# Encoder block on one core: x normalised once into resident fp16 parts that every input product reads

## The chip, the core and the metric

The kernel runs on one core of a Trainium2 chip. The time is the device time of one execution in microseconds (us). Engines are named as the profile names them: PE is the matrix engine (TensorE), PEld its weight loads, DVE the vector engine, ACT the scalar engine, POOL GpSimd, SP the engine that issues most of the DMA transfers. On-chip memory is SBUF; matmul results land in PSUM, of which a "bank" here holds 128x512 fp32.

## What is computed

x is (1, 1024 tokens, 1024 channels). In the reference, cut to the parts that matter here:

```
xn = rmsnorm(x, norm_gain)
q, k, v_kv, gate_a, u, v, gate_b, merge = split(xn @ w_in)   # 512,128,128,512,512,512,512,2048
a = block_attention(axial_rope(rms(q)), axial_rope(rms(k)), v_kv) * silu(gate_a)
g = gelu(u) * (W_s @ layernorm(gelu(v)) + b) * silu(gate_b)
y = sigmoid(merge_a) * (a @ w_proj_attn) + sigmoid(merge_b) * (g @ w_proj_gmlp)
out = rmsnorm(x + y @ w_out, final_gain)
```

Everything is fp32 at the borders. Nearly every product is made of three matmuls on split operands: each operand is cut into a high part and a low part (value minus high part), and hi*hi, hi*lo and lo*hi are summed in PSUM (`mm3`). The parts are either fp32r (a rounded fp32 form that the matrix engine takes in one pass) or fp16.

## The kernel before, in words

The tile scheduler orders the instructions of each engine; source order and priorities steer it. The stages, in order of their first matmul on PE:

- **kv** (192 matmuls, 256 columns wide). `load_x` brings the eight 512 KB chunks of x transposed (`xT`), and for each makes `xh` on ACT (L158, x times gain, rounded to fp32r) and `xl` on DVE (L159). These sixteen tiles stay resident and are the x operand of kv, v, q, u, gate a and gate b. They are x times gain but not divided by the row's root mean square: that factor (`rstd`) is applied to the products later.
- **rstd**. `add_square` (L171) loads x again in its natural layout (`xn`, 8 x 512 KB) and sums squares on ACT. DVE and POOL turn the eight sums into `rstd` (L133, L134), at 43.8 to 46.1 us.
- **v** and **q** (192 matmuls of 512 columns each, L174 to L176). Weights are split by `nat_weights` (ACT hi L112, DVE lo L118). v takes part in the scheduler's choice while kv still runs, as it needs no `rstd`.
- **sp**, the spatial products of the gMLP branch, key and query norm and rotation, transposes into `kT` and `qT`.
- **Attention** (first scores at 135.7 us): 64 score steps (PE L550/L551, DVE maximum L553, ACT exp L557, ACT and DVE splits L563/L564 into fp16, then a DMA transpose), 32 mixes `o` (L576, fp16), and between them 24 **fill** halves: u, gate a (`ga`) and gate b (`gb`), 24 matmuls of 512 columns each (L488 to L490). Their weights come through `stream_w`: ACT hi, POOL lo (L118). After each fill DVE multiplies by `rB` (a tile with 0.5*rstd of each token in all partitions) straight from PSUM (L494, L511), then the gate's function follows.
- **yb** (gMLP projection), with the forms for the next stage prepared beside it: `x_chunk` normalises x once more (rB on DVE, L765) and splits sums of quarters of it into fp16 pairs (seven per chunk, four chunks).
- **g** (merge gates, fp16, first matmul at 450.1 us). Its weights are scaled to unit size by `unit_scale`: tiny PE matmul `usg`, ACT copy L673, four POOL steps L674 to L677, then ACT splits L682.
- **out** and the final norm, to 735 us.

Of the kernel before, what the change touches and what calls it, by code (L numbers as in the profile page):

```python
# [30 lines left out]
def hybrid_block_kernel(  # L31
# [133 lines left out]
    ssx = const([P, NT], "ssx")

    def add_square(tt):

# [2 lines left out]
        act.activation(xn, xn, AF.Square, accum_out=ssx[:, tt:tt + 1])  # L171

    def mm3(o, ah, al, bh, bl, start, stop):
        pe.matmul(o, ah, bh, start=start, stop=False)  # L174
        pe.matmul(o, ah, bl, start=False, stop=False)  # L175
        pe.matmul(o, al, bh, start=False, stop=stop)  # L176
# [62 lines left out]
    gsc = const([P, 2], "gsc")
    dve.tensor_scalar(out=gsc[:, 0:1], in0=ssp[:, 16:17], scalar1=2.0 ** -16, scalar2=1e-30, op0=ALU.mult, op1=ALU.add)  # L240
    pool.tensor_tensor(out=gsc[:, 0:1], in0=gsc[:, 0:1], in1=mhalf[:, 0:1], op=ALU.pow)
    dve.reciprocal(gsc[:, 1:2], gsc[:, 0:1])
    dve.tensor_scalar(out=gs, in0=gain, scalar1=gsc[:, 0:1], scalar2=None, op0=ALU.mult)
    rstd = const([P, NT], "rstd")
    power_rstd(rstd, ssx, NT, 1.0 / D)
    bmh = const([P, 16], "bmh")
    dve.tensor_scalar(out=bmh, in0=cs[:, C_BM:C_BM + 16], scalar1=0.5, scalar2=None, op0=ALU.mult)
# [791 lines left out]
```

## Time and profile before

| what | value |
|---|---|
| median of 3 runs | 736.73 us (736.58 to 737.26) |
| the profiled execution's own time | 736.99 us |
| its span (first to last instruction) | 735.2 us, so 1.8 us lie outside |
| PE busy | 714.0 us of the span (97%), 4633 matmuls |
| DVE / ACT / POOL busy | 565.9 / 431.2 / 110.4 us |
| mean granted clock of PE | 0.992 |

A row of a group reads: line, engine, operation, output<-inputs, shape, count | busy us, mean ns of one | idle time before it and what released it. A row of the timeline reads: start, duration, engine, line, operation, output<-inputs, shape, count, and in brackets the idle time before it with the instruction that ended it. [...] A row of the windows view reads: the window, its length, busy us (and instructions) of PE, PEld, DVE, ACT, POOL, the granted clock as a share of full speed, the DMA share and GB/s.

### The profile page before, as it was taken

The page shows a single profiled execution, that of the slowest core. Times are in us where ns is not written, and L with a number is a line of the kernel's source. Part 1 is how long each engine was busy: PE and PEld are TensorE (multiplying, and loading weights), DVE is VectorE, ACT ScalarE, POOL GpSimd, SP SyncE. Part 2 cuts the span into 40 slices and gives each one's busy share as a digit, 9 for nine tenths or more (in the row PEclk, how much of TensorE's full clock was granted, in tenths as well). Part 3 has the DMA queues.
Part 4 walks back from the last instruction along what each step waited for, and adds up shares of the span by engine and source line. Part 5 has one row for each costly group of instructions (what it writes and reads, how often), then busy time and mean ns, then how long its engine had stood idle before and what let it go on. Part 6 is the DMA issues. An engine that isn't in the chain of part 4 may idle for free.

```text
span 735.2 us, 11836 instructions
## 1 busy us (share of the span) xinstructions
PE 714.0 (97%) x4633; PEld 531.4 (72%) x4633; DVE 565.9 (77%) x822; ACT 431.2 (59%) x770; POOL 110.4 (15%) x101
## 2 busy tenths in 40 slices
PE   8999999998999999999999996999999999999996
PEld 8978888776777788788887883465464556488885
DVE  6556868799797988878789999888887898952223
ACT  6634564685797887777784775654455536621011
POOL 0011223133132232213200003001101110000000
PEclk9999999999999999999999998999999999999999
DMA  8830301054889999998999500130121005440202
GB/s 307 317 129 1 115 16 43 1 122 94 150 157 182 176 180 167 183 170 175 154 245 287 132 30 14 45 129 15 46 98 58 0 1 184 157 146 1 114 30 86
DMA packets 152904, 85.59 MB, mean 116 GB/s; under 512 B 135440, under 2 KB 136080, under 8 KB 152848
## 3 DMA queue, kind: packets, MB, share of 16 engines
q1 hardware_dynamic: 152560, 84.56, 46.6%
q8 instruction: 36, 0.59, 0.3%
q10 hardware_dynamic: 288, 0.28, 0.1%
q14 instruction: 20, 0.16, 0.1%
HBM read 47.07 MB, written 4.19 MB: 70 GB/s over the span
## 4 chain that ended last, share of the span: by engine, by line
PE 83%; DVE 5%; ACT 5%; DMA 5%; issue 1%; POOL 1%; SPq 0%; POOLq 0%; ACTq 0%; DVEq 0%
PE o L576 5%; PE out L175 4%; DMA T<-p 4%; PE out L176 4%; PE out L174 4%; PE s L550 3%; PE s L551 3%; PE g L174 3%; PE g L175 3%; PE g L176 3%; PE gb L488 2%; PE q L174 2%; PE q L175 2%; PE v L175 2%; PE v L174 2%; PE q L176 2%
## 5 line engine op out<-in xcount | busy, mean ns | idle before, releaser
L564 DVE SCALAR_TENSOR_TENSOR p<-P,ri,p 128x1024 f16<-128x1024 f32 x64 | 83.4, 1304 | 26.4 <-ACT p L563 26.3
L557 ACT ACTIVATE P<-s,nm 128x1024 f32<-128x1024 f32 x64 | 71.2, 1113 | 24.2 <-DVE nm L553 20.8
L563 ACT ACTIVATE p<-P,ri 128x1024 f16<-128x1024 f32 x64 | 73.1, 1145 | 15.7 <-DMA T<-p 8.8
L553 DVE TENSOR_REDUCE nm<-s 128x1 f32<-128x1024 f32 x64 | 77.6, 1214 | 3.0 <-PE s L551 2.9
L576 PEld LDWEIGHTS <-vS 128*64 128x64 f16 x1536 | 45.3, 111 | 19.0 <-issue 17.8
L576 PE MATMUL o<-T,vS 128*64 128x128 f16 x1536 | 52.0, 222 | 4.2 <-DMA T<-p 3.8
L118 POOL TENSOR_TENSOR wl<-wraw,wh 128x512 fp32r<-128x512 f32 x24 | 39.9, 1665 | 97.7 <-ACT wh L112 55.6
L550 PE MATMUL s<-kT,qT 128*128 128x512 f32 x128 | 52.9, 413 | 0.0
L551 PE MATMUL s<-kT,qT 128*128 128x512 f32 x128 | 50.9, 397 | 0.0
L911 ACT ACTIVATE sq<-xr 128x1024 f32<-128x1024 f32 x7 | 7.4, 1062 | 65.4 <-DVE xr L969 65.4
L969 DVE TENSOR_TENSOR xr<-out,xr 128x1024 f32<-128x1024 f32 x7 | 8.6, 1224 | 47.6 <-PE out L176 47.5
L674 POOL TENSOR_SCALAR scg<-scg 128x1 f32<-128x1 f32 x8 | 6.5, 807 | 206.7 <-ACT scg L673 206.6
L550 PEld LDWEIGHTS s<-kT,qT 128*128 128x128 f32 x128 | 24.3, 189 | 6.3 <-issue 0.2
L551 PEld LDWEIGHTS s<-kT,qT 128*128 128x128 f32 x128 | 24.3, 190 | 5.4 <-issue 0.2
L112 ACT CAST wh<-wraw 128x512 fp32r<-128x512 f32 x35 | 21.4, 616 | 10.4 <-PE ga L489 3.4
L682 ACT ACTIVATE wg<-graw,scg 128x512 f16<-128x512 f32 x16 | 11.4, 721 | 26.6 <-PE g L176 13.2
L488 PE MATMUL ga<-xh,wh 128*128 128x512 f32 x64 | 26.0, 406 | 0.8 <-DVE ga30w L494 0.5
L488 PE MATMUL u<-xh,wh 128*128 128x512 f32 x64 | 25.8, 402 | 0.0
L488 PE MATMUL gb<-xh,wh 128*128 128x512 f32 x64 | 25.5, 399 | 0.0
L175 PE MATMUL yb<-gml,wh 128*128 128x512 f32 x64 | 25.5, 398 | 0.0
L490 PE MATMUL u<-xh,wl 128*128 128x512 f32 x64 | 25.4, 397 | 0.0
L490 PE MATMUL gb<-xh,wl 128*128 128x512 f32 x64 | 25.4, 396 | 0.0
(554 smaller groups left out, 2143.9 us busy)
## 6 DMA issues: line engine op xcount, KB each, us to landing
wraw<-in_wall_dram SPq DMA_DIRECT2D x59, 256.0 KB, 3.4
graw<-in_wall_dram SPq DMA_DIRECT2D x16, 512.0 KB, 5.8
xraw<-in_xT_dram SPq DMA_DIRECT2D x13, 512.0 KB, 6.4
xn<-in_x_dram SPq DMA_DIRECT2D x8, 512.0 KB, 6.3
wor<-in_wall_dram SPq DMA_DIRECT2D x8, 512.0 KB, 5.1
xr<-in_x_dram SPq DMA_DIRECT2D x8, 512.0 KB, 3.8
out_dram<-xr SPq DMA_DIRECT2D x7, 512.0 KB, 2.6
xraw<-in_xT_dram SPq DMA_DIRECT2D x5, 256.0 KB, 5.5
```

The source lines that it names most:

```text
L174: pe.matmul(o, ah, bh, start=start, stop=False)
L175: pe.matmul(o, ah, bl, start=False, stop=False)
L176: pe.matmul(o, al, bh, start=False, stop=stop)
L488: pe.matmul(o, wh[:, C(dt % 4)], xh[dt][:, H(h)], start=(dt == 0), stop=False)
L490: pe.matmul(o, wl[:, C(dt % 4)], xh[dt][:, H(h)], start=False, stop=(dt == 7))
L550: pe.matmul(sp[:, H(hf)], qs, kT[:, 2 * v, H(hf)], start=True, stop=False)
L551: pe.matmul(sp[:, H(hf)], qs, kT[:, 2 * v + 1, H(hf)], start=False, stop=True)
L553: dve.tensor_reduce(out=nm, in_=sp, axis=AX.X, op=ALU.max, negate=True)
L557: act.activation(Pt, sp, AF.Exp, bias=nm, accum_out=rsum)
L563: act.activation(hi, Pt, AF.Copy, scale=ri)
L564: dve.scalar_tensor_tensor(out=lo, in0=Pt, scalar=ri, in1=hi, op0=ALU.mult, op1=ALU.subtract)
L576: pe.matmul(ot[64 * h:64 * h + 64, 0:128], vS[:, kt, v, 64 * vl:64 * vl + 64], T[:, h, 8 * p + kt, :], start=(n == 0), stop=(n == len(part ...
```

## The change

x is divided by its row norm once, before v, and kept as fp16 hi and lo parts (`x16`, eight tiles). v, q, u, ga, gb, and three of the seven forms of the g stage read these parts. Only kv still uses the unnormalised fp32r parts, which now live in short rings (F and G, three tiles each) instead of staying.

- **Squares.** The natural-layout loads of x and their ACT squares go. The transposed chunks are squared instead, chunks 0 and 2 on POOL and six on ACT; POOL and DVE add them into two tiles; eight one-column matmuls (`sst`) sum over partitions. `rstd` follows as before, and `rB` is now made at once, by eight 128-column matmuls (`rb`) and an ACT copy.
- **norm_all.** Eight times: DVE multiplies a chunk of x by gain and rB (`raw_part`, 1024 wide), ACT casts it to fp16, DVE subtracts for the low part. The splits of v's weights go between.
- **Weights.** v, q and fill weights become fp16 as well, scaled to unit size first. v: 8 loads, 8 ACT squares, `usv`, ACT copy, POOL steps, then ACT hi and DVE lo. q the same. Fill weights: `all_scales` loads all 24 halves once for ACT squares, makes twelve scales in one go, and each half is loaded again later and split (ACT hi, DVE lo; POOL no longer takes part).
- **Order of v.** Products of chunks 0 to 5 for six token tiles in three banks, then chunks 6 and 7 for these, then tiles 6 and 7.
- **After the fills** the multiplication by rB goes: `silu2` reads PSUM directly with a scale, `uw` becomes a scaled copy. q's head norm uses one scale instead of per-token `rsq` and `rstd`.
- **g stage.** Forms "11", "22", "21" are taken from x16, so `x_chunk` makes four fp16 pairs per chunk instead of seven.

The diff, cut to its core:

```diff
+    def add_square(dt):
+        t = t4("T16", f"xsq{dt}")
+        if dt in (0, 2):
+            pool.tensor_tensor(out=t, in0=xraw0[dt], in1=xraw0[dt], op=ALU.mult)
+        else:
+            act.activation(t, xraw0[dt], AF.Square)
...
+    with tc.high_priority():
+        power_rstd(rstd, sst[:, 0:NT], NT, 1.0 / D)
+        dve.tensor_scalar(out=rstdh, in0=rstd, scalar1=0.5, scalar2=None, op0=ALU.mult)
+        rp = ps_s("rb")
+        for tt in range(NT):
+            pe.matmul(rp[:, C(tt)], rstdh[:, tt:tt + 1].broadcast_to([P, P]), identr.bitcast(F32), start=True, stop=True)
...
+    def norm_all():
+        def raw_part(dt):
+            dve.scalar_tensor_tensor(out=xraw0[dt], in0=xraw0[dt], scalar=gs[:, dt:dt + 1], in1=rB, op0=ALU.mult, op1=ALU.mult)
+
+        wv.extend(nat_split(dt, rv, wv16, scv) for dt in range(2))
+        act.copy(rB, rp)
+        raw_part(0)
+        for dt in range(8):
+            if dt < 7:
+                raw_part(dt + 1)
+            t = sb.tile([P, 2, 1024], F16, tag="xr", bufs=BUFS["xr"], name=f"x16{dt}")
+            ia = act.copy(t[:, 0, :], xraw0[dt])
+            iv = dve.tensor_tensor(out=t[:, 1, :], in0=xraw0[dt], in1=t[:, 0, :], op=ALU.subtract)
+            x16.append(t)
+            if dt < 6:
+                wv.append(nat_split(dt + 2, rv, wv16, scv))
...
+    for dt in range(6):
+        for c in range(6):
+            nat_part(vsp[c // 2][:, H(c % 2)], dt, c, wv[dt])
...
+    def all_scales():
...
+                raw = load_w(W_TR + base[o[0]] + int(o[1]), h)
+                act.activation(raw, raw, AF.Square, accum_out=ss[:, i, h:h + 1])
...
+    def prep(k, et):
...
+            raw = load_w(W_TR + base[k] + et, i)
+            split16(t[:, i, 0, :], t[:, i, 1, :], raw, sc[0], "dve")
...
-    def silu2(zp, h, name):
-        w = t2(f"{name}w")
-        dve.tensor_tensor(out=w, in0=zp, in1=rB[:, H(h)], op=ALU.mult)
+    def silu2(zp, sc, name):
         t = t2(f"{name}t")
-        act.activation(t, w, AF.Tanh)
-        dve.scalar_tensor_tensor(out=t, in0=t, scalar=1.0, in1=w, op0=ALU.add, op1=ALU.mult)
+        act.activation(t, zp, AF.Tanh, scale=sc)
+        dve.scalar_tensor_tensor(out=t, in0=t, scalar=1.0, in1=zp, op0=ALU.add, op1=ALU.mult)
```

How the order moves, at the place that matters most, the passage from kv to v. (L numbers of the changed kernel are those of its own file: mm3 is L187 to L189 there.) On PE before, at the first v matmul; `xh`, `xl` are parts of x, `nh`, `nl` parts of v's weights, `wh`, `wl` of kv's:

```order
L175 MATMUL kv_90<-wl_182,xh_210 128x256
L176 MATMUL kv_90<-wh_181,xl_211 128x256
L174 MATMUL kv_89<-wh_247,xh_240 128x256
L174 MATMUL kv_90<-wh_247,xh_240 128x256
L174 MATMUL v_488<-nh_383,xh_95 128x512
L175 MATMUL kv_89<-wl_248,xh_240 128x256
L176 MATMUL kv_89<-wh_247,xl_241 128x256
L174 MATMUL kv_89<-wh_247,xh_240 128x256
```

PE now, at the end of kv:

```order
L188 MATMUL kv_93<-wl_340,xh_371 128x256
L189 MATMUL kv_93<-wh_339,xl_372 128x256
L183 MATMUL sst<-ones,xsq_214 128x1 x8
L265 MATMUL usv<-ssv,mscale 128x1
L470 MATMUL wsum_688<-wspr_677,ones 128x512
L246 MATMUL rb<-identr,rstdh 128x128 x8
L187 LDWEIGHTS x_487
L187 MATMUL v_475<-wv_443,x_487 128x512
L188 LDWEIGHTS x_487
L188 MATMUL v_475<-wv_443,x_487 128x512
```

Before, v's first matmul stands in the middle of kv. Now all of kv comes first, then the small products for the sums of squares, the weight scale and rB, and only then v, whose fixed operand x_487 is the normalised x.

On DVE before, from the last `xl` on:

```order
L159 SCALAR_TENSOR_TENSOR xl_343<-xraw_341,cs,xh_342 128x1024
L118 TENSOR_TENSOR nl_384<-wraw_397,nh_399 128x512
L118 TENSOR_TENSOR nl_384<-wraw_405,nh_399 128x512
L118 TENSOR_TENSOR nl_415<-wraw_412,nh_414 128x512
L205 COPY vn<-kv_89 128x256
L118 TENSOR_TENSOR nl_415<-wraw_421,nh_414 128x512
L205 COPY vn<-kv_90 128x256
```

DVE now, from the first split of v's weights on; rows of the same kind follow for the other chunks:

```order
L276 SCALAR_TENSOR_TENSOR wv_443<-rawv_441,scv,wv_443 128x512 x2
L299 SCALAR_TENSOR_TENSOR xraw_97<-xraw_97,gs,rB 128x1024
L299 SCALAR_TENSOR_TENSOR xraw_138<-xraw_138,gs,rB 128x1024
L309 TENSOR_TENSOR x_487<-xraw_97,x_487 128x1024
L276 SCALAR_TENSOR_TENSOR wv_444<-rawv_441,scv,wv_444 128x512
L299 SCALAR_TENSOR_TENSOR xraw_175<-xraw_175,gs,rB 128x1024
L309 TENSOR_TENSOR x_493<-xraw_138,x_493 128x1024
L276 SCALAR_TENSOR_TENSOR wv_444<-rawv_441,scv,wv_444 128x512
L299 SCALAR_TENSOR_TENSOR xraw_216<-xraw_216,gs,rB 128x1024
```

Before, this passage holds splits of weights and copies of kv's result. Now it holds the normalisation of x chunk by chunk, two 1024-wide operations and one 512-wide one for each chunk.

On POOL before, after the identity matrix is made:

```order
L241 TENSOR_TENSOR gsc<-gsc,mhalf 128x1
L134 TENSOR_TENSOR rstd<-rstd,mhalf 128x8
L134 TENSOR_TENSOR rs_647<-rs_647,mhalf 128x1
L134 TENSOR_TENSOR rs_674<-rs_674,mhalf 128x1
L134 TENSOR_TENSOR rs_752<-rs_752,mhalf 128x1
```

POOL now:

```order
L169 TENSOR_TENSOR xsq_173<-xraw_97 128x1024
L199 TENSOR_TENSOR gsc<-gsc,mhalf 128x1
L169 TENSOR_TENSOR xsq_246<-xraw_175 128x1024
L175 TENSOR_TENSOR xsq_173<-xsq_173,xsq_246 128x1024
L268 TENSOR_SCALAR scv<-scv 128x1
L134 TENSOR_TENSOR rstd<-rstd,mhalf 128x8
L269 TENSOR_TENSOR scv<-scv,mhalf 128x1
L270 TENSOR_TENSOR scv<-scv 128x1
```

Before, POOL reaches `rstd` with nothing but one tiny operation ahead. Now three 1024-wide operations and the first step of v's weight scale (L268) stand ahead of it in its queue.

More of the change, by code (lines that the diff above doesn't have):

```diff
@@ L176, in mm3, with gain_scale @@
         pe.matmul(o, al, bh, start=False, stop=stop)
+    sst = ps_o("sst")
+    def gain_scale():
+        gsq = small("gsq")
+        act.activation(gs, gain, AF.Square, accum_out=gsq)
+        ssp = ps_z("ssx")
+        pe.matmul(ssp[:, 16:17], ones, gsq, start=True, stop=True)
+        dve.tensor_scalar(out=gsc[:, 0:1], in0=ssp[:, 16:17], scalar1=2.0 ** -16, scalar2=1e-30, op0=ALU.mult, op1=ALU.add)
+        pool.tensor_tensor(out=gsc[:, 0:1], in0=gsc[:, 0:1], in1=mhalf[:, 0:1], op=ALU.pow)
+        dve.reciprocal(gsc[:, 1:2], gsc[:, 0:1])
+        dve.tensor_scalar(out=gs, in0=gain, scalar1=gsc[:, 0:1], scalar2=None, op0=ALU.mult)
+        dve.tensor_scalar(out=bmh, in0=cs[:, C_BM:C_BM + 16], scalar1=0.5, scalar2=None, op0=ALU.mult)
+    gs = const([P, NT], "gs")
+    gsc = const([P, 2], "gsc")
+    bmh = const([P, 16], "bmh")
     kvs = [ps_s(f"kv{b}") for b in range(2)]
@@ L239, in hybrid_block_kernel @@
[L239 to L247, printed above, removed]
@@ new lines, in hybrid_block_kernel @@
+    rv = quads(("ptr", "ptr"), "rawv", F32)
+    wv16 = quads(("P", "P", "p16", "p16"), "wv16", F16)
+    ssv = nat_load(W_VIN, rv, "v")
+    with tc.high_priority(20):
+        scv = nat_scale(rv, ssv, wv16, "v")
+    scv2 = small("scv2")
+    dve.tensor_scalar(out=scv2, in0=scv[:, 1:2], scalar1=2.0, scalar2=None, op0=ALU.mult)
+    vsp = [ps_s(f"v{g}") for g in range(3)]
+    with tc.high_priority(), tc.manual_schedule(engines={dve.engine, act.engine}):
+        xlast = norm_all()
+    for dt in range(6):
+        for c in range(6):
+            nat_part(vsp[c // 2][:, H(c % 2)], dt, c, wv[dt])
@@ L462, in hybrid_block_kernel @@
     q_post(0, qsts[0])
+    v_finish(2)
+    prep_next()
     q_group(2)
     q_post(1, qsts[1])
+    v_finish(3)
+    prep_next()
     q_group(3)
-    rB = t4("rB", "rB")
-    for hh in range(2):
-        dg = t2(f"dg{hh}")
-        for k in range(4):
-            tt = 4 * hh + k
-            dve.tensor_scalar(out=dg[:, C(k)], in0=identr.bitcast(F32), scalar1=rstdh[:, tt:tt + 1], scalar2=None, op0=ALU.mult)
-        if hh == 0:
-            rp = ps_s("rb")
-        pe.matmul(rp[:, H(hh)], ones, dg, start=True, stop=True)
```

493 lines of the change are left out of this document (294 added, 199 removed).

## The prediction

> **What bounds the kernel now.** I read the profile's page first: busy time of the engines, then the chain that ended last.
>
> ```profile
> PE 714.0 (97%) x4633; PEld 531.4 (72%) x4633; DVE 565.9 (77%) x822; ACT 431.2 (59%) x770; POOL 110.4 (15%) x101
> PE 83%; DVE 5%; ACT 5%; DMA 5%; issue 1%; POOL 1%; SPq 0%; POOLq 0%; ACTq 0%; DVEq 0%
> ```
>
> PE is busy 97% of the span and is 83% of the chain. So what a matmul costs, and every time at which PE must wait, reaches the end; work on the others counts only where they come to lead. Where that may be, the windows show (columns: PE, PEld, DVE, ACT, POOL, clock, DMA share, GB/s).
>
> ```profile
> 20.00:40.00 20.00, 20.00 (x130) 18.02 (x130) 8.61 (x14) 12.87 (x23) 0.00 (x0) 1.00 0.83 294
> 40.00:60.00 20.00, 20.00 (x88) 16.15 (x87) 15.18 (x38) 7.64 (x13) 4.36 (x5) 1.00 0.25 85
> 60.00:80.00 20.00, 20.00 (x106) 17.20 (x105) 12.58 (x31) 9.58 (x16) 4.35 (x3) 1.00 0.14 42
> 80.00:100.00 20.00, 20.00 (x115) 17.47 (x114) 16.82 (x31) 13.00 (x21) 2.86 (x3) 1.00 0.22 71
> 100.00:120.00 20.00, 20.00 (x106) 17.05 (x105) 16.84 (x21) 11.31 (x18) 5.88 (x3) 1.00 0.10 33
> 120.00:140.00 20.00, 20.00 (x98) 15.97 (x97) 12.59 (x20) 8.53 (x17) 3.44 (x2) 1.00 0.04 14
> 140.00:160.00 20.00, 18.72 (x131) 15.03 (x130) 18.81 (x26) 16.86 (x33) 5.58 (x4) 1.00 0.36 80
> 160.00:180.00 20.00, 16.80 (x120) 12.62 (x119) 19.96 (x26) 11.96 (x25) 7.70 (x4) 1.00 0.62 119
> 180.00:200.00 20.00, 19.41 (x164) 15.17 (x164) 15.78 (x19) 15.23 (x32) 5.39 (x3) 0.91 0.67 120
> 220.00:380.00 160.00, 159.62 (x1632) 128.70 (x1631) 133.44 (x172) 127.34 (x235) 40.92 (x26) 1.00 0.97 178
> 400.00:450.00 50.00, 43.92 (x238) 35.68 (x236) 47.90 (x74) 34.68 (x66) 5.00 (x6) 0.96 0.32 93
> ```
>
> Three kinds of stretch. From 20 to 140 and from 220 to 380 PE never rests: a cheaper matmul is worth its full difference, a new wait costs its full length. From 140 to 180 PE lacks 4.5 us of 40 and DVE is busy 38.8: DVE leads. From 400 to 450 PE lacks 6.1 us and DVE is busy 47.9.
>
> The PE timeline shows the waits themselves: one for a transpose of the probabilities, one for the scale of the merge gate weights.
>
> ```profile
> 176.66 0.24 PE L576 MATMUL o<-T,vS 128*64 128x128 f16 x1
> 179.98 1.57 PE L576 MATMUL o<-T,vS 128*64 128x128 f16 x26 [3.08 <-DMA T<-p]
> 180.00:184.00 4.00, 4.00 (x48) 0.57 0.00 0
> 444.83 3.84 POOL L674 TENSOR_SCALAR scg<-scg 128x1 f32<-128x1 f32 x2 [67.10 <-ACT scg L673]
> 449.34 1.33 ACT L682 ACTIVATE wg<-graw,scg 128x512 f16<-128x512 f32 x2 [4.02 <-POOL scg L675]
> 450.11 0.61 PE L174 MATMUL g<-xf,wg 128*128 128x512 f16 x1 [6.20 <-ACT wg L682]
> ```
>
> After the 3.08 us wait, the next 4 us ran at a granted clock of 0.57 (third row): 43% of 4 us, 1.7 us, is lost on top of the wait.
>
> **Part 1: 960 matmuls go from fp32r to fp16.** Their number stays (192 v, 192 q, 24 x 24 fills). The timeline gives the distances:
>
> ```profile
> 86.40 0.39 PE L175 MATMUL q<-nl,xh 128*128 128x512 f32 x1
> 90.25 0.39 PE L174 MATMUL q<-nh,xh 128*128 128x512 f32 x1
> 327.31 0.50 PE L488 MATMUL gb<-xh,wh 128*128 128x512 f32 x1
> 327.64 0.39 PE L489 MATMUL gb<-xl,wh 128*128 128x512 f32 x1
> 332.65 0.40 PE L490 MATMUL gb<-xh,wl 128*128 128x512 f32 x1
> 559.77 0.38 PE L174 MATMUL g<-xfT,wg 128*128 128x512 f16 x1
> 561.93 0.38 PE L175 MATMUL g4T<-xfT,wg4T 128*128 128x512 f16 x1
> ```
>
> q: 17 steps in 3.85 us, 0.2265 each. A gate b fill, after its first: 22 steps in 5.01 us, 0.2277 each. Fp16 in the g stage: 10 steps in 2.16 us, 0.216. So at least 0.0105 x 384 = 4.0 us for v and q, 0.0117 x 576 = 6.7 us for the fills. More comes from the step after a change of type: 327.31 to 327.64 is 0.33, 0.1 over the rest, and a fill that follows an fp16 mix has no change any more; with some 40 such entries (24 halves, many cut in two by the order) that is 4.0. I take 5.0 for v and q (their rows are broken by narrower products and then step wider) and 10.7 for the fills, bounds 4.0 to 6.0 and 6.7 to 11. Of the fills a quarter lies before 200 us, where DVE leads; half of that quarter I count as lost: 9.4 remain.
>
> **Part 2: the passage from kv to v.** The rows of before that price it:
>
> ```profile
> 25.87 1.28 DVE L159 SCALAR_TENSOR_TENSOR xl<-xraw,cs,xh 128x1024 fp32r<-128x1024 f32 x1 [0.98 <-ACT xh L158]
> 33.41 0.28 PE L176 MATMUL kv<-wh,xl 128*128 128x256 f32 x1
> 43.78 0.17 DVE L133 TENSOR_SCALAR rstd<-ssx 128x8 f32<-128x8 f32 x1 [2.28 <-ACT xn L171]
> 44.03 2.03 POOL L134 TENSOR_TENSOR rstd<-rstd,mhalf 128x8 f32<-128x8 f32 x1 [32.97 <-DVE rstd L133]
> 46.09 0.17 DVE L249 TENSOR_SCALAR rstdh<-rstd 128x8 f32<-128x8 f32 x1 [0.94 <-POOL rstd L134]
> 135.22 1.02 PE L475 MATMUL rb<-dg,ones 128*128 128x512 f32 x2
> 135.68 0.79 PE L550 MATMUL s<-kT,qT 128*128 128x512 f32 x1
> 136.43 1.01 ACT L476 COPY rB<-rb 128x1024 f32<-128x1024 f32 x1
> L159 DVE SCALAR_TENSOR_TENSOR xl<-xraw,cs,xh 128x1024 fp32r<-128x1024 f32 x5 | 6.4, 1284 | 4.8 <-ACT xh L158 4.8
> L118 DVE TENSOR_TENSOR gml<-vm,gmh 128x1024 fp32r<-128x1024 f32 x4 | 4.8, 1217 | 0.0
> L159 DVE SCALAR_TENSOR_TENSOR xl<-xraw,cs,xh 128x512 fp32r<-128x512 f32 x5 | 3.7, 748 | 1.6 <-ACT xh L158 1.6
> ```
>
> Before, kv ended at 33.4 with v's matmuls mixed in; v needed no rstd, and rstd came at 46.1 while PE worked on. Now kv runs alone. The last chunk's `xl`, which ended at 27.2, allows its 24 narrow matmuls (about 3 us) to end at 30.5. Then follows a chain that nothing else on PE can cover: sst and usv, 0.5; POOL's first scale step, 0.5 (the row at 444.83 has 3.84 for two); rstd from DVE to DVE, 43.78 to 46.09, 2.3, and rstdh 0.2; rb, about 1; rB copy 1.0; first normalised chunk 1.3; its cast, 1.0 by the rB copy; weight splits ahead of rB on ACT some 1.0. The sum is 8.8 us, so v starts at about 39.3. rb stood at 135.2 before, so the 1 us is moved, not added; a wsum product fills 0.5. New idle time: 7.5 us. To it comes 1.7 us of low clock, as after the 3.08 us wait. Together +9.2; bounds +5 (POOL and weight steps hidden, clock kept) and +14 (POOL's step as slow as in the row at 444.83, squares of v's weights late on ACT).
>
> [...]
>
> After the start v needs 18 matmuls for each chunk, 3.9 us at 0.216; DVE delivers a chunk in 1.28 + 1.22 + 0.75 = 3.25 us. PE leads again, with little room.
>
> **Part 3: DVE on the way to the scores.** Before, DVE is busy 74.0 us from 40 to 140 (15.18 + 12.58 + 16.82 + 16.84 + 12.59). Added between v's start and the first maximum: eight chunks at 1.28 + 1.22, 20 us; eleven of the 24 fill halves' low parts (the order puts them ahead) at 0.75, 8.3; 4 more splits of v's weights, 3. Away go the eight `dg` scalings, under 2. That makes about 103 of the 101 us that PE needs for the same way (39.3 + 1.7 of clock + 60 of remaining work). DVE is as loaded as PE there. I charge 2.5 us; bounds 0, if the scheduler's order holds the low parts back well, and 8. The other additions are covered: 24 loads of 256 KB and their ACT squares fall into stretches where ACT is busy 7.6 to 13.0 of 20 us and the DMA share is 0.04 to 0.25; they would cost some 15 us of ACT if they weren't.
>
> **Part 4: attention and yb.** The removed POOL low parts and the removed multiplication by rB relieve DVE; from 220 to 380 PE is full anyway, so this gives nothing there by itself, and z, the fills' one bank, is held through the tanh now, which the order covers with scores or a mix. In the yb stretch 12 DVE subtractions and 12 casts go, but the 6.2 us end with POOL's chain behind the last yb copies, which stays: -0.5, bounds -2 and +2.
>
> Sum: -5.0 + 9.2 + 2.5 - 9.4 - 0.5 = -3.2. Against the profiled execution's 736.99 that is 733.8; that run is 0.26 over the median of 736.73, so 733.5.
>
> **The rivals.**
>
> *DVE and the passage lead to the scores (slower).* The mechanism is one: v can't start until x is normalised, DVE does that, and everything DVE has to do before the scores queues behind it. If v starts at 43 instead of 39.3 and DVE, loaded to about 100%, delivers the queries 5 us after PE is ready, the sum is -3.2 + 3.7 + 2.5 = +3.0: 739.7. It decides from 3.2 us over my charge. For it: the 103 us against 101; DVE at 19.96 of 20 from 160 to 180. Against it: relief later on, in just the stretch where DVE led. Chance 0.27.
>
> *The fills' gain is swallowed (no change).* If attention follows the transposes or DVE and not PE, the fills keep about 6.2 of 9.4, and the sum is 0: 736.7. For it: DMA share 0.97 from 220 to 380. Against it: PE's 159.62 of 160 there, which no waiting engine has. Chance 0.13.
>
> *The passage is cheap.* If the small products and weight scale hide, v starts at 36 and no clock is lost: 3.3 + 1.7 less, and DVE charges 1.0 instead of 2.5: -9.7, 727.0. Chance 0.2. My forecast has the remaining 0.4.
>
> **How the numbers follow.** The likeliest is 733.5, its own range 730 to 736. With the bounds of the passage (-4, +5) and of DVE (-2.5, +5.5) the range becomes 724 to 744: it leaves out part of the cheap passage and the worst of the first rival, some 0.2. A measurement can tell 0.2%, 1.5 us, from no change. Faster by more: forecast 0.38, cheap passage 0.2: 0.58. Same: the swallowed gain and edges, 0.14. Slower: 0.28.
>
> **What would show it.** The step between v, q and fill matmuls at 0.216 (right), or still 0.227 (part 1 wrong). PE idle between the last kv and the first v: 7 to 8 us, with a clock under 0.7 behind it; under 4 or over 12 would be a rival. The first scores at 141 against 135.7: 138 or less is the cheap passage, 145 or more the first rival, and DVE full from 40 to 140 its sign. Scores to the last fill shorter by 9: if it is shorter by 6 or less, the gain was swallowed. The wait ahead of g within 2 us of 6.2. The prediction is wrong if another stretch than these moves the time by over 3 us.

## The result, and the profile after

The changed kernel takes 756.88 us (median of four runs, 755.64 to 758.65) against 736.98 us of the kernel before on the same chip: ratio 1.0272, 95% interval 1.0250 to 1.0295. It is 19.9 us slower. The forecast was 733.5 us, 724 to 744, so it was wrong in sign and outside its range. The profiled execution is the slowest of the four, 758.65 us; its span is 756.9 us.

The page of the changed kernel, busy time and chain. PE's share falls from 97% to 95%, and the chain now goes through DVE and ACT for 12% each (5% before): PE waits more often.

```profile
PE 716.4 (95%) x4667; PEld 453.8 (60%) x4667; DVE 592.8 (78%) x841; ACT 460.0 (61%) x838; POOL 84.1 (11%) x89
PE 64%; DVE 12%; ACT 12%; DMA 6%; issue 4%; POOL 1%; SPq 0%; POOLq 0%; DVEq 0%; ACTq 0%
```

Its windows, in the columns used in the prediction. Before, PE was full from 20 to 140 and from 220 to 380, with the clock at 1.00, and lacked 3.2 us from 160 to 180. Now it lacks 1.1, 3.7, 4.8, 4.5, 2.9 and 3.7 us in these rows, and the clock falls to 0.83 in three of them. (The last row holds the wait ahead of g, which the kernel before has too.)

```profile
20.00:40.00 20.00, 18.87 (x151) 17.96 (x150) 13.12 (x17) 12.45 (x28) 1.89 (x3) 0.99 0.67 249
40.00:60.00 20.00, 16.27 (x68) 8.60 (x69) 17.10 (x20) 11.36 (x14) 0.94 (x3) 0.83 0.00 0
100.00:120.00 20.00, 15.18 (x73) 8.44 (x72) 12.23 (x26) 15.01 (x31) 4.34 (x5) 0.83 0.44 139
160.00:180.00 20.00, 15.52 (x77) 8.51 (x78) 18.36 (x28) 17.88 (x37) 3.26 (x2) 1.00 0.41 114
220.00:240.00 20.00, 17.12 (x115) 9.76 (x113) 16.93 (x23) 14.69 (x30) 3.74 (x3) 0.97 0.56 142
460.00:480.00 20.00, 16.34 (x71) 9.45 (x69) 13.41 (x18) 14.41 (x29) 3.12 (x4) 0.83 0.15 53
```

Its view of waits, PE alone (sum us, times, longest). Five of these rows belong to things that the change put in ahead of the scores: the measured fill scales (khi), the passage to v (x, rstdh), the squares beside kv (wl, xl). The other two, P and uw, lie in attention; a wait of scores for P is new there, too.

```profile
PE s L712 <- ACT P L719: 5.4, 4, 1.9
PE ktp L561 <- ACT khi L112: 4.7, 1, 4.7
PE v L187 <- ACT x L308: 3.5, 1, 3.5
PE ga L646 <- DVE uw L668: 3.1, 1, 3.1
PE kv L188 <- DVE wl L118: 2.4, 1, 2.4
PE kv L189 <- DVE xl L159: 1.9, 2, 1.1
PE rb L246 <- DVE rstdh L243: 1.3, 1, 1.3
```

Set out by stages (start of the named matmul in the profiled executions, us):

| kernel | last kv | first v | first scores | first g | end of span |
|---|---|---|---|---|---|
| before | 33.41 | 19.23 | 135.68 | 450.11 | 735.2 |
| after | 35.56 | 47.09 | 155.95 | 469.19 | 756.9 |
| fill_scale_const | 36.19 | 48.14 | 149.50 | 462.01 | 749.3 |
| no_pool_squares | 31.61 | 38.26 | 145.66 | 458.07 | 746.1 |
| no_rb_chain | 33.41 | 33.53 | 145.03 | 458.19 | 744.6 |
| all_three_gone | 32.52 | 32.64 | 139.49 | 451.26 | 738.2 |
| gone_no_fill_lo | 32.53 | 32.65 | 138.56 | 438.65 | 724.9 |
| const_scale_no_lo | – | – | 152.47 | 452.28 | 739.7 |
| before_fp16 | 30.97 | 18.01 | 128.72 | 438.08 | 726.1 |

Of after minus before, +20.3 us arise before the first scores, −1.2 us from the scores to g, and +2.6 us from g to the end. So there are two questions: what cost 20 us in front, and where the gain of the cheaper fill steps went.

### The profile page after: what moved, and what is told of

Read it like the earlier page. It is cut to its first block, busy times and chain, and to the rows that moved or that the text cites. A ratio compares the mean times of both kernels' runs of the same rounds, so it can differ in the third digit from the quotient of the medians.

```text
span 756.9 us, 11985 instructions
## 1 busy us (share of the span) xinstructions
PE 716.4 (95%) x4667; PEld 453.8 (60%) x4667; DVE 592.8 (78%) x841; ACT 460.0 (61%) x838; POOL 84.1 (11%) x89
## 4 chain that ended last, share of the span: by engine, by line
PE 64%; DVE 12%; ACT 12%; DMA 6%; issue 4%; POOL 1%; SPq 0%; POOLq 0%; DVEq 0%; ACTq 0%
PE out L188 4%; PE out L189 4%; PE out L187 4%; DMA wraw<-in_wall_dram 3%; PE o L738 3%; PE g L187 3%; PE g L188 3%; PE g L189 3%; DVE p L726 3%; DVE nm L715 2%; DMA T<-p 2%; ACT P L719 2%; PE yb L187 2%; PE yb L188 2%; PE yb L189 2%
## 5 line engine op out<-in xcount | busy, mean ns | idle before, releaser
L712 PE MATMUL s<-kT,qT 128*128 128x512 f32 x128 | 56.1, 438 | 7.2 <-ACT P L719 5.4
L738 PEld LDWEIGHTS <-vS 128*64 128x64 f16 x1536 | 46.1, 111 | 17.7 <-issue 16.5
L713 PE MATMUL s<-kT,qT 128*128 128x512 f32 x128 | 50.4, 394 | 0.0
L187 PE MATMUL g<-x,wg 128*128 128x512 f16 x96 | 37.4, 389 | 0.5 <-ACT wg L275 0.5
L188 PE MATMUL g<-x,wg 128*128 128x512 f16 x96 | 37.3, 389 | 0.0
L189 PE MATMUL g<-x,wg 128*128 128x512 f16 x96 | 36.9, 384 | 0.0
L268 POOL TENSOR_SCALAR scg<-scg 128x1 f32<-128x1 f32 x8 | 5.4, 672 | 212.7 <-ACT scg L267 131.6
L187 PE MATMUL v<-wv,x 128*128 128x512 f16 x64 | 25.0, 391 | 3.5 <-ACT x L308 3.5
L646 PE MATMUL ga<-x,wa 128*128 128x512 f16 x64 | 25.0, 391 | 3.1 <-DVE uw L668 3.1
L275 ACT ACTIVATE wg<-graw,scg 128x512 f16<-128x512 f32 x16 | 11.4, 721 | 26.2 <-PE g L189 12.8
L187 PE MATMUL q<-wq,x 128*128 128x512 f16 x64 | 25.4, 397 | 1.0 <-ACT vm L382 0.8
L187 PE MATMUL yb<-gmh,wh 128*128 128x512 f32 x64 | 25.4, 400 | 0.0
L189 PE MATMUL out<-wo,yhl 128*128 128x512 f32 x64 | 25.4, 396 | 0.0
```

The costliest lines, as they stand in the source:

```text
L275: act.activation(hi, raw, AF.Copy, scale=sc)
L646: pe.matmul(o, wh, x16[dt][:, 0, H(h)], start=(dt == 0), stop=False)
L712: pe.matmul(sp[:, H(hf)], qs, kT[:, 2 * v, H(hf)], start=True, stop=False)
L713: pe.matmul(sp[:, H(hf)], qs, kT[:, 2 * v + 1, H(hf)], start=False, stop=True)
L738: pe.matmul(ot[64 * h:64 * h + 64, 0:128], vS[:, kt, v, 64 * vl:64 * vl + 64], T[:, h, 8 * p + kt, :], start=(n == 0), stop=(n == len(part ...
```

## The experiments

The theory after reading the trace was that three additions in front cost the time, each by its own wait: the fill scales' squares in ACT's queue, POOL's squares beside DVE, and the chain from kv to v. The rival was that DVE's added work as a whole sets the pace, so that removing one wait would only show the next. A second pair concerned attention: DVE's low parts of the fill weights, or their later loads.

**Fill scales by a constant.** No squares and no first load of the fill weights; the scale is 1024.

```diff
-                raw = load_w(W_TR + base[o[0]] + int(o[1]), h)
-                act.activation(raw, raw, AF.Square, accum_out=ss[:, i, h:h + 1])
+        dve.memset(s0, 1024.0)
```

> The changed kernel, but the twelve scales of the fill weights are a constant instead of being measured: the 24 loads and 24 ACT squares ahead of the scores are gone, the rest stays. Theory A (the squares wait for their loads in ACT's queue, and the key's cast and the copies of q stand behind them; PE's 4.66 us ahead of the key transposes is that): that wait and its 1.7 us of low clock go, 6 to 9 us less than the changed kernel's 756.9, so 748 to 751, first scores by 150 instead of 156. Theory B (DVE's load sets the way to the scores, the waits are only where it shows): DVE's work is unchanged, so 755 or more.

Measured 751.17 us (750.79 to 752.17), ratio 1.0193 [1.0178, 1.0208]: 5.7 us of the 19.9. First scores come at 149.50 and not 155.95, and the wait for khi is gone. The time lies 0.2 us above the range of theory A. How these squares held PE can be read in the changed kernel. ACT's groups from 72 to 112 us: 23 squares take 14.4 us, the reads of their sums 4.3, and ACT stands idle 8.4 us in front of them, waiting for loads.

```profile
L581 ACT ACTIVATE wraw<-wraw 128x512 f32<-128x512 f32 x23 | 14.4, 628 | 8.4 <-DMA wraw<-in_wall_dram 8.1
L581 ACT ACTIVATION_READ_ACCUMULATOR wraw<-wraw 128x1 f32 x23 | 4.3, 189 | 0.0
```

The timeline of the three engines there: DVE ends the rotated key `kn` at 104.4, but ACT casts it at 108.45, after a square that itself waited for its load. PE needs the cast at 104.9 and gets it 4.66 us later. The last row is PE's window from there: the clock is 0.50.

```profile
103.15 1.22 DVE L413 TENSOR_TENSOR kn<-kn,ktmp 128x1024 f32<-128x1024 f32 x1
107.83 0.63 ACT L581 ACTIVATE wraw<-wraw 128x512 f32<-128x512 f32 x1 [0.64 <-DMA wraw<-in_wall_dram]
108.45 1.03 ACT L112 CAST khi<-kn 128x1024 fp32r<-128x1024 f32 x1
109.53 0.75 PE L561 MATMUL ktp<-identr,khi 128*128 128x128 f32 x4 [4.66 <-ACT khi L112]
109.00:114.00 5.00, 4.31 (x13) 0.50 0.37 130
```

**POOL's squares away.** Chunks 0 and 2 are not squared or added, so the sum of squares lacks them.

```diff
         if dt in (0, 2):
-            pool.tensor_tensor(out=t, in0=xraw0[dt], in1=xraw0[dt], op=ALU.mult)
+            ssq.append(None)
+            return
```

> The changed kernel without the squares of chunks 0 and 2 and their addition on POOL and on DVE (the sums cover six of eight chunks). Theory A (POOL beside DVE stretches DVE's low parts of x, 1.83 us where 0.75 was usual, and kv waits for them, 4.3 us in three waits and a lower clock): kv ends at 30 to 31.5 instead of 35.6, and the time falls by 4 to 5 us to 752. Theory B (DVE's total load sets the way): 1.2 us less, one DVE addition, so 755.5.

Measured 748.75 us (747.89 to 750.57), ratio 1.0167 [1.0147, 1.0186]: −8.1 us, 3 us more than theory A allowed. kv ends 4.0 us sooner, and the way from kv to v shrinks from 11.5 to 6.65 us: the one-column products of the sums (`sst`) now run before kv ends, and rb follows without a wait. In the changed kernel, the first DVE rows of kv:

```profile
7.02 1.83 DVE L159 SCALAR_TENSOR_TENSOR xl<-xraw,cs,xh 128x512 fp32r<-128x512 f32 x1 [1.40 <-ACT xh L158]
9.11 0.74 DVE L159 SCALAR_TENSOR_TENSOR xl<-xraw,cs,xh 128x512 fp32r<-128x512 f32 x1
10.66 1.77 DVE L201 TENSOR_SCALAR gs<-cs,gsc 128x8 f32<-128x8 f32 x1
12.35 4.20 DVE L159 SCALAR_TENSOR_TENSOR xl<-xraw,cs,xh 128x512 fp32r<-128x512 f32 x3
```

and POOL's in the same time:

```profile
6.41 1.90 POOL L169 TENSOR_TENSOR xsq<-xraw 128x1024 f32<-128x1024 f32 x1 [5.11 <-DMA xraw<-in_xT_dram]
10.51 1.90 POOL L169 TENSOR_TENSOR xsq<-xraw 128x1024 f32<-128x1024 f32 x1
12.49 2.85 POOL L175 TENSOR_TENSOR xsq<-xsq,xsq 128x1024 f32<-128x1024 f32 x1
```

Without POOL's squares the same DVE operations take:

```profile
6.16 0.75 DVE L159 SCALAR_TENSOR_TENSOR xl<-xraw,cs,xh 128x512 fp32r<-128x512 f32 x1 [0.17 <-ACT xh L158]
9.70 0.21 DVE L197 TENSOR_SCALAR gs<-cs,gsc 128x8 f32<-128x8 f32 x1
9.82 2.07 DVE L159 SCALAR_TENSOR_TENSOR xl<-xraw,cs,xh 128x512 fp32r<-128x512 f32 x3
```

An operation on eight columns took 1.77 us instead of 0.21; it ended at 12.43, when POOL's square ended (10.51 + 1.90 = 12.41). The 1.83 us `xl` ended 0.54 us after POOL's first square (8.31), where a whole undisturbed one takes 0.75. So both were held up while POOL ran, the first to the end of POOL's square; by what in the hardware, no run shows.

**The squares on ACT instead.** Same sums, other engine: ACT squares chunks 0 and 2, DVE adds them.

```diff
-            pool.tensor_tensor(out=t, in0=xraw0[dt], in1=xraw0[dt], op=ALU.mult)
+            act.activation(t, xraw0[dt], AF.Square)
```

> The changed kernel with all eight squares on ACT and both additions on DVE, so POOL has nothing there and the whole of the sums is kept. Theory A (POOL's presence beside DVE stretched the low parts of x): DVE's 512-wide low parts take 0.75 us again, kv's three waits nearly go, kv ends by 32.5, 750 to 752; 2 us more than without these squares at all, for ACT's 2.1 and DVE's 1.2 us. Rival (it is the work itself, not its place): 755 or more.

Measured 753.76 us (752.64 to 754.44), ratio 1.0222 [1.0205, 1.0239]: −3.1 us. kv ends at 32.08 and `xl` is back at 0.75, so POOL was what slowed kv; but the way from kv to v keeps 11.7 us. Moving the squares off POOL wins 3.1 of the 8.1 us, less than theory A asked; the other 5.0 go only when the work goes too.

**No chain from kv to v.** rB is set to 0.5, and v's and q's weight scales to constants: v depends on no sum of squares.

```diff
-            pe.matmul(rp[:, C(tt)], rstdh[:, tt:tt + 1].broadcast_to([P, P]), identr.bitcast(F32), start=True, stop=True)
+        dve.memset(rB, 0.5)
...
-            act.activation(dst[dt][:, 0, :], raws[dt], AF.Square, accum_out=ss[:, dt:dt + 1])
+        dve.memset(sc[:, 0:1], 1024.0)
```

> The changed kernel with rB a constant (no rb products, no copy; x is divided by no row norm) and constant scales for the weights of v and q (no squares of them): v waits neither for rstd nor for a scale, and the normalisation runs beside kv. Theory A (the passage from kv to v is a chain of small steps on PE, DVE, POOL, ACT: 11.5 us between the last kv and the first v): v starts within 2 us after kv, 10 to 12 us less with the clock, so 745 to 747. Theory B (the normalisation's DVE work of 25 us has to be done anyhow ahead of the scores): 3 to 5 us less, 752 to 754, and PE waits later instead, between v's chunks or ahead of the scores.

Measured 748.33 us (746.14 to 752.65), ratio 1.016 [1.0119, 1.0201]: −8.5 us. v starts right behind kv, 13.6 us earlier than in the changed kernel, but the first scores come only 10.9 us earlier, since PE now waits for DVE on the way. The time lies between the two theories. (kv ends 2.15 us sooner here as well, although POOL's squares stay, so the three edits in front are not independent of one another.) Two of these waits, after v's first row:

```profile
33.53 0.39 PE L187 MATMUL v<-wv,x 128*128 128x512 f16 x1
35.02 0.39 PE L189 MATMUL v<-wv,x 128*128 128x512 f16 x1 [0.88 <-DVE x L305]
38.01 2.67 PE L183 MATMUL sst<-ones,xsq 128*128 128x1 f32 x16 [1.52 <-DVE xsq L177]
```

**The clock in the passage alone.** Eight products that nobody reads, after rb, while PE waits for the first chunk.

```diff
+        for i in range(8):
+            pe.matmul(wp[:, 0:P], rstdh[:, 0:1].broadcast_to([P, P]), identr.bitcast(F32), start=True, stop=True)
```

> The changed kernel with eight more 128-column products behind rb whose result nobody reads, so that PE isn't idle in the 3.5 us before the first v matmul. Theory E (this wait's clock costs 1.4 to 2 us on top): v runs at 0.216 a step from its start, granted clock near 1.00 in the window 47 to 51 instead of about 0.55, and the time is 1 to 2 us under 756.9. Rival (v is paced by DVE's chunks anyhow, so a cold start is caught up): clock up, time within 0.5 us of the changed kernel's.

Measured 754.47 us (754.30 to 754.69), ratio 1.0233 [1.0218, 1.0248]: −2.4 us. PE's window 47 to 51 in this kernel:

```profile
47.00:51.00 4.00, 4.00 (x20) 1.00 0.00 0
```

In the changed kernel the same window has 0.57 (shown further below). v itself starts only 0.6 us earlier (46.47), the first scores 2.9 (153.04): most of the gain is clock.

**All three gone.** The edits of fill_scale_const, no_pool_squares and no_rb_chain (there without any squares) together.

> The three together: no measured scales for any weights, no POOL squares, constant rB. Theory A: the gains add up, some 20 to 25 us, so 732 to 737, first scores at 135 or earlier, since v and q in fp16 remain faster. Theory B: DVE leads once the waits are gone, and the sum is 12 us or less, 745 or more, with DVE busy 19 of 20 us from 40 to 120.

Measured 739.13 us (737.88 to 740.88, ten runs), ratio 1.0028 [1.0017, 1.004]: −17.8 us, where the three alone add up to 22.3. The front is 16.5 us shorter. Neither theory had the time: with the scores at 139.49 it misses A by 2 us and B by 6. So these three hold nearly all of the loss, and yet this kernel, which computes none of the scales, is still not faster than before: the fills' gain isn't there.

**Low parts of the fill weights left out, on top.** The third product of each step reads the high part again, so that PE has the same number of steps; DVE's 24 subtractions go.

```diff
-            split16(t[:, i, 0, :], t[:, i, 1, :], raw, sc[0], "dve")
+            act.activation(t[:, i, 0, :], raw, AF.Copy, scale=sc[0])
```

> The kernel with all three gone (739.1 us), and also without the low parts of the fill weights on DVE: 24 subtractions of 0.66 to 0.75 us, the fills' third matmul reads the high part again, so PE's work is the same and the low part's share of the result is left out. Open is why scores to g takes 311.8 us there, only 2.7 less than before, though fills and scores together are faster. Theory C (DVE leads in the early attention, the low parts, which POOL made before, are what delays the maxima and queries): the waits of PE between scores and g, 16.4 us, fall to 11 or less, the time to 732 to 735. Theory D (the order of the queues on ACT and the length of the chain from scores to transpose set these waits): no more than 2 us less, 737 to 739.

Measured 726.26 us (725.17 to 726.94), ratio 0.9849 [0.9831, 0.9867]: 12.9 us less again, nearly all of it (11.7 us) between scores and g. That is more than theory C asked. PE is full in this kernel in the window where the changed one lacked 2.9 us:

```profile
220.00:240.00 20.00, 20.00 (x227) 12.68 (x222) 18.18 (x25) 16.07 (x31) 2.55 (x2) 1.00 0.90 183
```

**The subtraction without its load.** In all_three_gone, DVE subtracts from rB, which has long been there, and not from the loaded weights: the same number and width of operations, other data. The second operand is still ACT's high part, which ACT makes from the loaded weights; so DVE no longer holds the load's buffer, but it can still not start before the load.

```diff
+            dve.scalar_tensor_tensor(out=t[:, i, 1, :], in0=rB[:, H(i)], scalar=sc[0], in1=t[:, i, 0, :], op0=ALU.mult, op1=ALU.subtract)
```

> The kernel with all three gone (739.1 us), but DVE makes the 24 low parts of the fill weights from rB, which lies in SBUF, and not from the loaded weights, so the number and width of DVE's operations is kept while they wait for no load and hold no load buffer (the low parts hold no weights then). Theory C (DVE's work itself, 24 x 0.7 us): 737 to 740, like all three gone. Theory F (DVE's queue stands still for the loads and for the buffers of the ring): 726 to 730, like the kernel without low parts.

Measured 740.46 us (739.08 to 741.34), ratio 1.0053 [1.0036, 1.007], against 739.13 of all_three_gone: nothing is gained. So holding the load's buffers is not what the low parts cost. That waiting for the loads isn't either, this run can't show, but the trace of all_three_gone does: the 24 subtractions take 19.5 us of DVE, and DVE never stands idle ahead of one.

```profile
L270 DVE SCALAR_TENSOR_TENSOR wb<-wraw,wsc,wb 128x512 f16<-128x512 f32 x8 | 6.8, 871 | 0.0
L270 DVE SCALAR_TENSOR_TENSOR wa<-wraw,wsc,wa 128x512 f16<-128x512 f32 x8 | 6.8, 870 | 0.0
L270 DVE SCALAR_TENSOR_TENSOR wu<-wraw,wsc,wu 128x512 f16<-128x512 f32 x8 | 5.9, 740 | 0.0
```

What is left is DVE's time, or its place in DVE's queue.

**The same omission in the changed kernel alone.** Low parts left out, everything else as in the change.

> The changed kernel without the low parts of the fill weights on DVE (the fills' third matmul reads the high part), everything else kept: measured scales, squares on POOL, the rB chain. Theory C says DVE leads from the normalisation to the middle of the attention, so that its 24 x 0.7 us count even with the waits at the start in place: 744 to 748, 9 to 13 less than 756.9. Rival (with the early waits in place these hide the low parts, and DVE only led once they were gone): 752 or more.

Measured 758.50 us (754.15 to 760.07), ratio 1.0272 [1.0236, 1.0308]: no gain at all. The theory as I then had it, that DVE's low parts alone take the fills' gain in the changed kernel, falls. Something else stands in the same place; the next run shows what.

**Constant fill scales and no low parts.** The two edits, the front's other costs left in.

> The kernel with constant fill scales (751.2 us), and without the low parts of the fill weights on DVE; squares on POOL and the rB chain stay. Alone the missing low parts gave nothing in the changed kernel (758.5) and 12.9 us where all three were gone. Theory I (the measured scales push all splits of fill weights against the first scores, twelve ACT casts from 136 to 167 us, so ACT and the order hold the attention there whatever DVE does; without them DVE's low parts are what is left): 738 to 741, the stretch from scores to g 12 us shorter than the 312.5 with constant scales. Rival J (the gain belongs to the other two, the squares and the rB chain): 748 or more.

Measured 740.02 us (738.13 to 741.66, six runs), ratio 1.0048 [1.0026, 1.007]: 11.2 us under fill_scale_const, 18.5 under no_fill_lo_alone. From scores to g it takes 299.8 us, where fill_scale_const has 312.5, no_fill_lo_alone 314.0 and the changed kernel 313.2. So the measured scales and the low parts hide one another: each alone leaves attention as it is, both together free 13 us. The traces show where they meet. With measured scales, ACT can cast the fill weights only once the scales are there: 16 of the 24 casts lie between 136 and 167 us in the changed kernel, around its first scores (155.95), and between 137 and 159 in no_fill_lo_alone. With the constant they lie between 73 and 117 us (fill_scale_const), long before the scores. The window 220 to 240 of no_fill_lo_alone:

```profile
220.00:240.00 20.00, 16.59 (x139) 9.80 (x139) 16.32 (x23) 16.02 (x30) 3.58 (x2) 0.91 0.64 145
```

of fill_scale_const:

```profile
220.00:240.00 20.00, 17.34 (x104) 9.66 (x102) 17.15 (x23) 16.21 (x30) 3.59 (x2) 0.83 0.64 146
```

and of const_scale_no_lo, where alone of the three PE is full:

```profile
220.00:240.00 20.00, 20.00 (x174) 11.50 (x174) 19.03 (x25) 19.80 (x38) 2.57 (x2) 1.00 0.90 201
```

**Low parts on POOL.** fill_scale_const with scale 1 and POOL subtracting, as before the change.

```diff
-            split16(t[:, i, 0, :], t[:, i, 1, :], raw, sc[0], "dve")
+            split(t[:, i, 0, :], t[:, i, 1, :], raw, act, pool)
```

> The kernel with constant fill scales (751.2 us), but with the low parts of the fill weights on POOL, as they were in the kernel before, with scale 1; DVE is relieved of 24 x 0.7 us. Theory C (DVE's load in early attention): 3 to 5 us less, 746 to 748. Theory A's other side (POOL beside DVE stretches DVE's operations, as at the start): 751 or more, DVE's 512-wide operations longer while POOL runs, and the norms' POOL steps wait behind the low parts.

Measured 753.40 us (752.31 to 754.54), ratio 1.0222 [1.02, 1.0245], 2.2 us more than fill_scale_const. From scores to g it is 9.6 us shorter (302.9 against 312.5), but the first scores come 10.3 us later (159.78): POOL relieves DVE in attention and takes it back in front, where it slows DVE again: DVE's eight splits of q's weights take 1.24 us each there, and 0.74 in fill_scale_const.

**yb's weights held back.** The scheduler moves loads and splits of the gMLP projection's weights up to 223 to 230 us, where ACT waits for them while scores wait for ACT. Here they may not start before mix 26.

```diff
-        hi, lo = stream_w(W_PROJ + dt, 1, act, dve)
+        with tc.issue_after(ilate.ins):
+            hi, lo = stream_w(W_PROJ + dt, 1, act, dve)
```

> The changed kernel, with nothing but the same holding back of the yb weights; all that is computed is kept. Theory K: PE's waits of 0.98 and 1.9 us at 234 to 237 and their clock go, 3 to 5 us less, 752 to 754. Rival: 756 or more.

> The kernel with all three gone (739.1 us), with the splits of the yb weights held back until mix 26 of 32; there three of them had been pulled ahead to 209 us, where ACT waits for their loads and the exponentials stand behind them. Theory K (that is what PE's waits of 1.45 and 1.9 us at 216 to 219 and the low clock behind them come from): these waits go, 3 to 5 us less, 734 to 736. Rival (theory C, DVE's low parts): the waits stay or move, 738 to 740.

In the changed kernel: 753.85 us (753.27 to 755.59), ratio 1.0247 [1.0219, 1.0276], 3.0 us less; the intervals of the two ratios overlap, but every run lies below every run of the changed kernel. In all_three_gone: 738.68 us (735.82 to 741.77, eight runs), ratio 1.0036 [1.0009, 1.0063], against 739.13 no difference that can be told. A small cost of the changed kernel, and not the reason why the fills' gain is missing. The rows on ACT and, last, on PE in the changed kernel:

```profile
227.49 0.62 ACT L112 CAST wh<-wraw 128x512 fp32r<-128x512 f32 x1 [0.76 <-DMA wraw<-in_wall_dram]
228.66 0.62 ACT L112 CAST wh<-wraw 128x512 fp32r<-128x512 f32 x1 [0.55 <-DMA wraw<-in_wall_dram]
237.17 0.50 PE L712 MATMUL s<-kT,qT 128*128 128x512 f32 x1 [1.90 <-ACT P L719]
```

**The number form alone, in the kernel before.** x's parts and the weights' parts of kv, v, q and the fills become fp16 instead of fp32r; no norm ahead of v, no scales, no other order in the source.

```diff
-        hi = t4("xh", f"xh{dt}", F32R)
-        lo = t4("xl", f"xl{dt}", F32R)
+        hi = t4("xh", f"xh{dt}", F16, (P, 2048))[:, 0:1024]
+        lo = t4("xl", f"xl{dt}", F16, (P, 2048))[:, 0:1024]
```

> The kernel before, with nothing but the type of the split parts changed: x times gain, and the weights of kv, v, q and fills, become fp16 high and low parts instead of fp32r (no scales, no early normalisation, no new loads; kv too). This is the first part of the prediction alone. Theory G (the narrower type alone gives its full step where PE leads, and everything that was lost came with the normalisation and the scales): 1152 matmuls are faster by 0.01 to 0.018, so 12 to 17 us less than 737, 720 to 725, less up to 3 us where DVE leads from 140 to 180. Rival H (PE's faster steps only turn into waits for DVE, ACT or transposes in the attention, as in the changed kernel): 728 to 734.

Measured 727.32 us (726.12 to 728.23), ratio 0.987 [0.9855, 0.9885]: 9.7 us less than before and 29.6 less than the changed kernel, so it beats both. First scores come 7.0 us sooner, the stretch to g is 5.1 us shorter, and from g to the end it is 2.9 us longer. Theory G had asked for more; the time is 0.7 us under the range of rival H, and as H said, faster steps turn into waits in part: in attention the DMA share is now 1.00, and PE lacks 7.1 us of 160 where it lacked 0.4 before:

```profile
220.00:380.00 160.00, 152.87 (x1620) 95.14 (x1618) 133.96 (x171) 128.39 (x236) 36.27 (x23) 0.99 1.00 182
```

## Why the prediction was wrong, point by point

**Part 1, the cheaper steps: right in kind.** It asked for 0.216 us. Two fill steps of the changed kernel, 20 apart:

```profile
215.12 0.39 PE L646 MATMUL u<-x,wu 128*128 128x512 f16 x1
219.45 0.38 PE L648 MATMUL u<-x,wu 128*128 128x512 f16 x1
```

4.33 us for 20, 0.2165. (The rows' own 0.39 and 0.38 us are longer: by its row a step starts before the one ahead of it ends, so what it costs on a busy PE is read from start to start.) By itself the form gave −9.7 us in before_fp16, of the −14.4 that I took for v, q and fills (kv, which that kernel changes too, included). So at most two thirds reach the end.

**kv's end: a cost that the sum lacks.** I took the end of kv from DVE's undisturbed `xl` and put it at 30.5 us; it was 35.6. POOL's squares beside DVE stretched the `xl`, and PE waited 0.84, 1.10 and 2.37 us inside kv. The change part did list the squares on POOL; I priced POOL's place in the queue for rstd and not what POOL does to DVE. The failed step is "allows its 24 narrow matmuls (about 3 us) to end at 30.5". Runs no_pool_squares (31.61) and squares_on_act (32.08) show it: 4.0 of the 5.1 us go with POOL's squares, and the last 1.1 were simply put too low.

**Part 2, the passage: the chain was right, its small products were not.** Forecast 8.8 us, measured 11.4. Of these PE idles 4.8 (1.32 and 3.50), where I had named 7 to 8; the other 6.6 are PE's own small products. PE's timeline of the changed kernel:

```profile
35.56 0.28 PE L189 MATMUL kv<-wh,xl 128*128 128x256 f32 x1
35.68 1.84 PE L183 MATMUL sst<-ones,xsq 128*128 128x1 f32 x16
37.78 1.12 PE L470 MATMUL wsum<-wspr,ones 128*128 128x512 f32 x2
40.23 3.36 PE L246 MATMUL rb<-identr,rstdh 128*128 128x128 f32 x16 [1.32 <-DVE rstdh L243]
47.09 0.39 PE L187 MATMUL v<-wv,x 128*128 128x512 f16 x1 [3.50 <-ACT x L308]
```

and its windows over these rows, PE alone (busy, instructions, clock, DMA share, GB/s):

```profile
36.00:40.00 4.00, 2.87 (x18) 1.00 0.01 2
40.00:44.00 4.00, 3.36 (x16) 0.59 0.01 2
47.00:51.00 4.00, 3.91 (x11) 0.57 0.00 0
```

The mis-sized terms are the small products. sst and usv were put at 0.5 and take 2.1, from 35.68 to wsum's start. rb was put at 1.0, from a row that shows two of the four matmul instructions of the old rb, 512 columns wide and at full clock (all four take 1.3 us, from 134.36 to the scores). The new rb is sixteen instructions of 0.21 each, 3.36, and runs at a clock of 0.59, which costs 41% of it, 1.4 us; in no_pool_squares the same sixteen take 1.95. POOL's and the weight steps cost less than feared: of the way over POOL to rstd only the wait of 1.32 is left, behind the 1.1 us of wsum, and from rb to v it is 3.50 where the terms gave 4.3. The 1.7 us of low clock behind v's start held: 0.57 over 4 us, and warm_passage wins 2.4 us by keeping it at 1.00. What I had missed is that the clock falls twice.

Behind the wait of 3.50 us most of v's steps in that window are 0.43 us apart instead of 0.2165; in no_pool_squares and late_yb, behind the same wait, they are too. But the 0.59 under rb follows a wait of 1.32 us only, behind small products: on these rows the small products did not keep the clock up. In late_yb the sixteen of rb come behind the same products and the same 1.32 us and take 2.05, not 3.36; so what decides there is not shown. The lower bound of the passage (clock kept) and the cheap passage (no clock lost) took it that the clock holds behind v's start. No run shows that for a gap left open: 1.00 was measured there in warm_passage, where products fill the wait.

**Part 3, the way to the scores: the sentence "are covered" failed.** From the first v to the first scores I had 101.7 us (39.3 to 141) and measured 108.9. The 7.2 us between are about the wait for khi, 4.66, and half of the 5 us behind it, which run at clock 0.50: 2.5. In fill_scale_const the same way takes 101.4 us, and DVE is busy 97.2 of 100 us from 48 to 148, PE 99.0: DVE is as loaded as forecast and holds PE up little, while the fill scales were sized wrongly. That 101.4 meets 101.7 so well is in part luck: my terms gave 103.1, and the 101 us that I set against DVE's 103 was no sum of work, since it adds the time at which v starts, 39.3, to what follows. I had judged ACT by its busy share per window, 7.6 to 13.0 of 20 us, and the price of "some 15 us of ACT if they weren't" treated the squares as work that can wait. But on these rows ACT kept the order of its queue: after the key was ready at 104.4 it stood 0.89 and 0.64 us for the loads of squares, with the key's cast behind them.

The front's error against the 141 us that I named is then whole: 5.1 (kv) + 2.7 (passage) + 7.2 (key) = 15.0, and the scores came at 155.95. (141 was itself 1.4 us below what my terms gave, 135.7 + 6.7 = 142.4; and in the passage 8.8 less 1.0 and 0.5 is 7.3 of idle time, not 7.5.)

**Part 4 and the fills' gain: wrong.** I expected the way from scores to g shorter by 9; it was shorter by 1.2. The steps did shrink (fills and scores together 200.9 to 192.6 us, summed from start to start), but waits rose from 12.3 to 17.1 us, and the transposes of q added 1.5. The step that failed is the sentence "The removed POOL low parts and the removed multiplication by rB relieve DVE". It took the relief of POOL for a relief of DVE; in fact DVE took the low parts over, 19.0 us in the changed kernel. And "from 220 to 380 PE is full anyway" did not hold: PE lacks 2.9 us from 220 to 240. The test that I had named, 6 or less, says that the gain was swallowed. Why the low parts and the measured scales each hide the other's cost is settled only in part. Where they meet is shown: the scales push 16 casts of fill weights to the first scores, and the low parts follow these casts on DVE. Which queue then holds each of PE's waits is not shown; only the pair was shown to matter (const_scale_no_lo, gone_no_fill_lo).

**yb and g.** I forecast −0.5; from g to the end it was +2.6. The wait ahead of g did not stay within 2 us of 6.2: it is 3.04 us ahead of the weight scale and 0.6 behind it.

```profile
467.39 0.58 PE L265 MATMUL usg<-gss,mscale 128*128 128x1 f32 x2 [3.04 <-ACT gsq L971]
468.14 0.59 PE L265 MATMUL usg<-gss,mscale 128*128 128x1 f32 x2 [0.17 <-ACT gsq L971]
469.19 0.61 PE L187 MATMUL g<-x,wg 128*128 128x512 f16 x1 [0.46 <-ACT wg L275]
```

That gain lies before g and is part of the −1.2. Behind g, 1.0 us of the +2.6 is clock: 0.87 over the first 20 us, where the kernel before had 0.92 over its first 20. Most of the rest lies in PE's steps and not in waits, which come to 0.2 us behind g; its cause stays open. The +2.9 of before_fp16 is another thing: there PE waits 3.3 us behind g, most of it for DVE.

**The rivals.** The slower one, DVE and the passage, went the right way, at 739.7 us, and its mark, scores at 145 or later, was met; v came at 47.09 where it had 43. But its other mark, DVE full from 40 to 140, was not: DVE is busy 17.1 and 12.2 of 20 us in the two windows shown. What came late was ACT's queue and kv, which it did not have. The swallowed gain came true as well. I had set the two side by side as alternatives; they came together, and neither alone reaches the 756.88 that was measured.

**The sum as a whole.** The profiled spans differ by +21.7 us where the sum had −3.2, so 24.9 us are to be found. By my own terms 13.6 of them lie ahead of the scores (155.95 against 142.4) and 11.3 behind (+1.4 against −9.4 and −0.5). (The lower end of the range, 724, is 3 us below what the two bounds named for it give.)

## What to carry to other kernels

Price an added operation by the queue that it enters, not by the share of time in which that engine is free: in this kernel a row of squares, with the loads that they waited for, held up one cast behind them, and PE waited 4.66 us for it. An operation moved to an idle POOL was not free here, where DVE works in the same microseconds (a 128x512 `xl` took 1.83 us and not 0.75); look at DVE's own rows before and after. And try a change's cheapest part alone: the fp16 form, without the norm, scales and order that came with it, gave 9.7 us, where the whole lost 19.9.

## What the runs showed of the hardware

- A DVE operation on 128x8 took 1.77 us beside a POOL square and 0.21 without; a 128x512 `xl` 1.83 and 0.75.
- Eight 128-column products with fp32 operands ran as sixteen matmul instructions and took 3.36 us at a clock of 0.59, and 1.95 in no_pool_squares. At 0.59 each costs as much as a 512-column fp16 step at full clock (0.2165).
- A stretch of one-column and other small products was followed by a clock of 0.59, with no wait longer than 1.32 us in it; in late_yb, behind the same products and wait, the sixteen instructions that follow took 2.05 us and not 3.36.
- A granted clock of 0.57 over 4 us after a wait of 3.50 us became 1.00 when eight unread products filled the wait but for 1.38 us.
